# A second gate's modulation moved beside the output projection, and more seven-product pairs in a feed-forward block

## The chip, the cores and the metric

The kernel runs on one core of one Trainium2 chip. The metric is device time in microseconds (us) of one execution of the whole program. A core has a matrix engine (TensorE, "PE" in the profile, with its weight loads as "PEld"), a vector engine (VectorE, "DVE"), a scalar engine (ScalarE, "ACT"), GpSimd ("POOL") and SyncE ("SP"), which here does nothing but issue transfers. Each engine works through its own list of instructions in a fixed order, and engines wait for one another through semaphores.

## The reference

One decoder layer on 256 rows of width 2048, all in 32-bit floats. The parts that matter here:

```python
mod = jax.nn.silu(c) @ w_ada[l] + b_ada[l]
shift1, scale1, gate1, shift2, scale2, gate2 = jnp.split(mod[:, None, :], N_MOD, axis=-1)
h = rms_norm(x, norm1_gain[l]) * (1 + scale1) + shift1
x = x + gate1 * mixing_sublayer(h, ..., w_out[l])      # ends in  y @ w_out
h = rms_norm(x, norm2_gain[l]) * (1 + scale2) + shift2
gate, up = jnp.split(h @ w_ffn_in, 2, axis=-1)         # w_ffn_in is 2048 x 11264
x = x + gate2 * ((jax.nn.silu(gate) * up) @ w_ffn_out) # w_ffn_out is 5632 x 2048
```

`c` is one vector of 2048 numbers, `w_ada` is 2048 x 12288: each of the six segments of `mod` (here `gate2`) is a product of a vector with a 2048 x 2048 block of `w_ada`, 16 MB that are read once.

## The kernel before

**Products.** A 32-bit product is made of three passes of TensorE: both operands are split into a rounded high part and a low rest, and `mm3` (L163 to L166) adds high x high, high x low and low x high in the same PSUM bank. A pass takes a 128 x 128 stationary tile of the activations and streams 512 columns of weights. The 256 rows are two tiles `t` of 128.

**Weights.** `load_weights` (L135) brings two 128-row tiles of weights at a time, 512 KB, into one of four `raw` buffers (issued from SP, L146); ScalarE casts it to the high part `whi` (L158), VectorE subtracts to make the low part `wlo` (L159). There are four `whi` and four `wlo` buffers, and a caller may name further `spare` tiles. `block` (L168) then runs one column block of 512 over all row tiles of the weights. Where a block is called with `tiles=(0,)` and then `tiles=(1,)`, the weights of the whole block have to be there by the end of its first half.

**Background.** A segment of `mod` is done on VectorE: 32 loads of 128 x 1024 of `w_ada` into tiles of a ring (`ring["tags"]`), each followed by one multiply-add ("mac", L289, 128 x 1024). `tick` hands these out: `block` calls it at every second row tile with the number in `state["rate"]`, so a rate of 0.65 means 0.65 loads and macs per 512 KB of weights. A mac is recorded when the ring is full, behind the last `wlo` split recorded so far. `biased` (L366) clears the sum on GpSimd and puts the bias row into it.

**Order of the stages** around the change: mixing branches (`y_block`); the output projection with `w_out`, four blocks of 512 columns, the fourth one tile at a time, with `residual` (gate1 times the block, plus `x`), and the norm of the second half (`norm2_rows`, `norm2_turn`, its transposes at L1199); eleven feed-forward units, each 512 columns of `gate` and 512 of `up`; the output of the feed-forward, in a first pass over columns 0 to 1023 (`OUT_A`), a second pass over columns 1024 to 2047 (`OUT_B`), and plain blocks for the rows that the second pass leaves. Weights are loaded under `prio()`, that is, the planner that makes the fixed order prefers them to work recorded earlier without it.

**Seven-product pairs.** `fast_products` (L1328) takes two column blocks and pairs of row tiles. A plain pair is 2 x 2 x 2 = 8 products (24 passes). A pair marked 1 in the order list is done as a 2 x 2 block product with seven products (21 passes): sums and differences of the weights are made on VectorE (L1312) in two tiles of `tags`, each of them split like weights (L1309), and sums of the activations are made once beforehand (`sums_of_h2`, `sums_of_unit`, L1272). The units in `FAST` have three such pairs of eight, `OUT_A` has six of 22, `OUT_B` six of 14. `sums_of_unit(n)` (L1462) adds high and low part of one unit's activation (L1466), makes four sums (L1272) and splits them (L1470, L1471), in the tiles `AR0` and `AR1`; it is called at steps 2, 4 and 6 of the first pass.

**gate2** is appended to the background after the last fast unit, so it runs beside units 8, 9 and 10; what is left is flushed at step 7 of the first pass. `parts_of_gate2` and `rows_of_gate2` (L1483, L1489) spread it over all partitions near the end of that pass. The residual `x2` is written to memory after the projection (`put_away`) and read back at steps 8 to 11 of the first pass (`bring_back`).

## Time and profile before

| | us |
|---|---|
| median of 3 runs | 1591.57 |
| lowest, highest | 1590.14, 1591.96 |
| the profiled execution: its own time | 1590.96 |
| the profiled execution: span of the profile | 1589.2 |

Where stages lie in that span, from the timeline: the output projection from about 782 to 872, its fourth block from 848.6; unit 0 from 873; the fast units 1 to 7 from about 919 to 1216; units 8 to 10 to about 1350; the first output pass to 1468.5; the second to about 1541; the end at 1589.

The page gives busy time and share of the span by engine, then groups of instructions: the line, engine, operation, `out<-in` with the tiles' names, the shape, a count, and behind the bar the busy time, the mean duration of one in ns, and the idle time of the engine just ahead of them with what ended it. A row of the timeline is start, duration, engine, line, operation and names, with the idle time before it in brackets. A row of the windows is the stretch, its length, the busy time of PE, PEld, DVE, ACT and POOL with counts, the granted clock of TensorE, the mean busy share of the 16 DMA engines, and GB/s. A transfer's row is its count, its size and the median us from issue to landing. Passes of TensorE overlap: the duration of one is longer than the time from one start to the next.

### The profile page before, as it was taken

The page shows a single profiled execution, that of the slowest core. Times are in us where ns is not written, and L with a number is a line of the kernel's source. Part 1 is how long each engine was busy: PE and PEld are TensorE (multiplying, and loading weights), DVE is VectorE, ACT ScalarE, POOL GpSimd, SP SyncE. Part 2 cuts the span into 40 slices and gives each one's busy share as a digit, 9 for nine tenths or more (in the row PEclk, how much of TensorE's full clock was granted, in tenths as well). Part 3 has the DMA queues.
Part 4 walks back from the last instruction along what each step waited for, and adds up shares of the span by engine and source line. Part 5 has one row for each costly group of instructions (what it writes and reads, how often), then busy time and mean ns, then how long its engine had stood idle before and what let it go on. Part 6 is the DMA issues. An engine that isn't in the chain of part 4 may idle for free.

```text
span 1589.2 us, 20174 instructions
## 1 busy us (share of the span) xinstructions
PE 1577.6 (99%) x7243; PEld 1304.6 (82%) x7243; DVE 1299.3 (82%) x1556; ACT 852.6 (54%) x1195; POOL 11.2 (1%) x22
## 2 busy tenths in 40 slices
PE   9999999999999999999999999999999999999998
PEld 7878888888888888888887888888888888888887
DVE  6889996888888686877756689999997677998884
ACT  5654448775764444444445756555554434455552
POOL 1000000000000000000000000000000000000000
PEclk9999999999999999999999999999999999999999
DMA  9999997677788899988767566666668789866664
GB/s 334 360 328 322 333 305 241 212 229 231 231 267 271 300 300 324 307 278 298 230 206 244 174 195 189 198 202 196 206 191 279 259 290 311 275 193 219 201 207 138
DMA packets 195740, 400.16 MB, mean 252 GB/s; under 512 B 13038, under 2 KB 28052, under 8 KB 195640
## 3 DMA queue, kind: packets, MB, share of 16 engines
q1 hardware_dynamic: 194664, 396.70, 75.9%
q0 software_dynamic: 800, 2.11, 0.3%
q8 instruction: 57, 0.93, 0.2%
q14 instruction: 43, 0.35, 0.1%
q10 hardware_dynamic: 176, 0.07, 0.0%
HBM read 394.63 MB, written 4.19 MB: 251 GB/s over the span
## 4 chain that ended last, share of the span: by engine, by line
PE 88%; DVE 4%; ACT 3%; DMA 3%; issue 2%; SPq 0%; ACTq 0%; DVEq 0%
PE acc L166 22%; PE acc L165 21%; PE acc L164 21%; PE misc L165 6%; PE misc L166 6%; PE misc L164 5%; DMA raw<-w_in 2%; PE acc L443 1%; ACT whi L158 1%; DVE wlo L159 1%; DMA raw<-w_br_gla 1%; DVE wlo L1309 1%; PE misc L812 1%; PE misc L1122 1%; ACT scr L638 1%
## 5 line engine op out<-in xcount | busy, mean ns | idle before, releaser
L158 ACT CAST whi<-raw 128x1024 fp32r<-128x1024 f32 x362 | 368.5, 1022 | 406.0 <-PE acc L166 270.2
L159 DVE TENSOR_TENSOR wlo<-raw,whi 128x1024 fp32r<-128x1024 f32 x362 | 425.6, 1183 | 186.8 <-ACT whi L158 184.8
L164 PE MATMUL acc<-whi,H 128*128 128x512 f32 x1245 | 487.3, 392 | 1.2 <-ACT H L455 0.8
L165 PE MATMUL acc<-wlo,H 128*128 128x512 f32 x1245 | 486.3, 391 | 0.8 <-DVE wlo L159 0.7
L166 PE MATMUL acc<-whi,H 128*128 128x512 f32 x1245 | 486.0, 391 | 0.4 <-DVE H L462 0.4
L166 PEld LDWEIGHTS acc<-whi,H 128*128 128x128 f32 x1245 | 233.6, 188 | 50.7 <-DVE H L462 1.6
L164 PEld LDWEIGHTS acc<-whi,H 128*128 128x128 f32 x1245 | 233.7, 188 | 50.0 <-ACT H L455 1.3
L165 PEld LDWEIGHTS acc<-wlo,H 128*128 128x128 f32 x1245 | 233.9, 188 | 48.6 <-DVE wlo L159 1.7
L1308 ACT CAST whi<-raw 128x1024 fp32r<-128x1024 f32 (+1 forms) x148 | 142.0, 974 | 100.4 <-PE acc L166 37.0
L1309 DVE TENSOR_TENSOR wlo<-raw,whi 128x1024 fp32r<-128x1024 f32 (+1 forms) x148 | 162.8, 1122 | 10.9 <-ACT whi L1308 9.5
L165 PE MATMUL acc<-wlo,A 128*128 128x512 f32 x222 | 86.5, 390 | 0.8 <-DVE wlo L159 0.8
L164 PE MATMUL acc<-whi,A 128*128 128x512 f32 x222 | 87.0, 392 | 0.0
L166 PE MATMUL acc<-whi,A 128*128 128x512 f32 x216 | 84.1, 389 | 0.0
L289 DVE SCALAR_TENSOR_TENSOR ada<-AR,csil,ada 128x1024 f32<-128x1024 f32 x51 | 64.8, 1278 | 1.8 <-DMA AR<-w_ada 1.6
L164 PE MATMUL misc<-whi,H 128*128 128x512 f32 x158 | 61.7, 391 | 0.0
L165 PE MATMUL misc<-wlo,H 128*128 128x512 f32 x158 | 61.6, 390 | 0.0
L166 PE MATMUL misc<-whi,H 128*128 128x512 f32 x158 | 61.5, 389 | 0.0
L165 PEld LDWEIGHTS acc<-wlo,A 128*128 128x128 f32 x222 | 41.7, 188 | 9.5 <-DVE wlo L159 1.1
L164 PEld LDWEIGHTS acc<-whi,A 128*128 128x128 f32 x222 | 41.7, 188 | 8.6 <-ACT whi L158 0.3
L1308 ACT CAST A<-raw 128x1024 fp32r<-128x1024 f32 (+1 forms) x36 | 34.9, 982 | 25.5 <-DMA raw<-w_ffn_in 9.1
L1308 ACT CAST whi<-AR 128x1024 fp32r<-128x1024 f32 x24 | 25.3, 1053 | 42.1 <-PE misc L166 20.6
L166 PEld LDWEIGHTS acc<-whi,A 128*128 128x128 f32 x216 | 40.6, 188 | 8.5
(487 smaller groups left out, 2306.3 us busy)
## 6 DMA issues: line engine op xcount, KB each, us to landing
raw<-w_in SPq DMA_DIRECT2D x205, 512.0 KB, 5.0
raw<-w_ffn_in SPq DMA_DIRECT2D x176, 512.0 KB, 4.6
raw<-w_ffn_out SPq DMA_DIRECT2D x88, 512.0 KB, 5.1
AR<-w_ada SPq DMA_DIRECT2D x70, 512.0 KB, 5.0
raw<-w_out SPq DMA_DIRECT2D x32, 512.0 KB, 4.8
KC<-w_ada SPq DMA_DIRECT2D x26, 512.0 KB, 5.3
OS<-w_ada SPq DMA_DIRECT2D x16, 512.0 KB, 6.5
KD<-w_ada SPq DMA_DIRECT2D x16, 512.0 KB, 5.5
```

Source lines behind the costliest of these rows:

```text
L158: state["cast"] = nc.scalar.copy(hi[:, :n, :], raw[:, :n, :])
L159: state["split"] = nc.vector.tensor_tensor(lo[:, :n, :], raw[:, :n, :], hi[:, :n, :].bitcast(F32), op=ALU.subtract)
L164: nc.tensor.matmul(ps, lh, rh, start=start, stop=False, skip_group_check=seeded)
L165: nc.tensor.matmul(ps, lh, rl, start=False, stop=False, skip_group_check=seeded)
L166: state["mm"] = nc.tensor.matmul(ps, ll, rh, start=False, stop=stop, skip_group_check=seeded)
L289: nc.vector.scalar_tensor_tensor(acc, raw, c, acc, op0=ALU.mult, op1=ALU.add)
L443: state["warm"] = nc.tensor.matmul(ps, ones_r, wide, start=True, stop=True)
L638: nc.scalar.activation(junk, heads(b)[:, t, h, :], AF.Square, accum_out=ss[:, t, i : i + 1])
L812: nc.tensor.matmul(ps[:n, t * N_GLA + h, :].rearrange("p (s l) -> p s l", l=L), at(f, h, t)[:, :n], odd(at(f, h, t)), start=True, stop=True,)
L1122: nc.tensor.transpose(ps[:, i, :], src[:, i * P : (i + 1) * P], ident)
L1308: nc.scalar.copy(hi[:, :n, :], src)
L1309: state["split"] = nc.vector.tensor_tensor(lo[:, :n, :], src, hi[:, :n, :].bitcast(F32), op=ALU.subtract)
```

## The change

- The background work for `gate2` starts at the beginning of the output projection instead of after the last fast unit, at a rate of 0.68. Its sum lies in `OS0` and `T3` instead of `ada`; its ring is `A12`, `KD`, `KC` and at first `H7`, then `T0`. Through the fourth projection block and the first block of unit 0, which go one tile at a time, the rate is halved or nothing (`pace`). The finished sum is written to memory before the first fast unit and read back at step 7 of the first output pass.
- Units 2 to 10 are fast instead of 1 to 7: nine instead of seven.
- The second output pass has 18 pairs, eight of them fast, instead of 14 with six. It needs the activation sums of unit 3 as well, made at the last step of the first pass. The plain remainder is 8 row tiles instead of 16, and the last block has no spare tiles.
- Tiles move accordingly: the scratch tiles of the output passes are `AR0`, `A8`; the activations of units 8 and 9 lie elsewhere; spare tiles of the fourth projection block and of unit 0 are others; two quarters of `x2` come back after the second pass is recorded.

```diff
-RATE_IN, RATE_MID, RATE_FFN = 0.8, 0.6, 0.65
-RATE_OUT = 2.5
+RATE_IN, RATE_MID, RATE_LATE = 0.8, 0.6, 0.68
...
-FAST = range(1, 8)
-OUT_UNITS = (4, 5, 6)
+FAST = range(2, 11)
+OUT_UNITS = (4, 5, 6, 3)
...
-OUT_B = ((0, 0), (1, 0)) + tuple(x for i in range(6) for x in ((8 + i, 1), (2 + i, 0)))
+OUT_B = ((0, 0), (1, 0)) + tuple(x for a, b in zip((8, 9, 10, 11, 12, 13, 6, 7), (2, 3, 4, 5, 14, 15, 16, 17)) for x in ((a, 1), (b, 0)))
...
     def block(...
-              steps=None):
+              steps=None, pace=None):
...
+        if pace is None:
+            pace = 1.0 if tiles[-1] == NT - 1 else 0.0
         for k in range(k0, k1):
-            if (k - k0) % 2 == 0 and tiles[-1] == NT - 1:
-                tick(state["rate"])
+            if (k - k0) % 2 == 0:
+                tick(state["rate"] * pace)
...
-            hf = S(("KC", "T6")[j - 2], [P, 4, P]) if t == 0 and j >= 2 else scr([P, 4, P])
+            hf = S(("OD", "T6")[j - 2], [P, 4, P]) if t == 0 and j >= 2 else scr([P, 4, P])
...
-    def bring_back(n):
-        x2[n] = S(X2_TAGS[n], [P, NT, NB])
+    def bring_back(n, tag):
+        x2[n] = S(tag, [P, NT, NB])
...
+    gate2_away = [away.tile([P, 2 * NB], F32, tag=f"gate2_{j}", name=nm("gate2")) for j in range(2)]
+
+    def gate2_bg():
+        acc = biased([S(tag, [P, 2 * NB]) for tag in ("OS0", "T3")], SEG_GATE2)
+        yield from ada_segment_steps(acc, SEG_GATE2, None, False)
+        yield from last_macs()
+        for j in range(2):
+            nc.gpsimd.dma_start(gate2_away[j], acc[j])
+
+    state["rate"] = RATE_LATE
+    ring["tags"] = ("A12", "KD", "KC", "H7")
+    bg.append(gate2_bg())
...
-    w = load_weights(I["w_out"], 0, KC, 3 * NB, spare=("T0", "T3", "OS0", "OS1", "OS2", "OD", "A7", "A11"))
-    flush()
+    w = load_weights(I["w_out"], 0, KC, 3 * NB, spare=("T0", "AR0", "AR1", "OS1", "OS2", "OD", "A7", "A11"))
+    ring["tags"] = ("A12", "KD", "KC")
+    while SEG_SCALE2 not in mod2:
+        tick(1)
...
-        block({t: ps}, y_at, None, 0, KC, 0, w=w, tiles=(t,), steps={N2_AT[0]: lambda: norm2_turn(0, xs)} if t else None)
+        block({t: ps}, y_at, None, 0, KC, 0, w=w, tiles=(t,), steps={N2_AT[0]: lambda: norm2_turn(0, xs)} if t else None,
+              pace=0 if t else 0.5)
...
-             "OS0", "OS1", "OS2", "OD", "KD", "H0", "H1"]
+             "ada", "ada", "AR1", "A4", "H0", "H1"]
...
-    state["rate"] = RATE_FFN
-    ring["tags"] = ("AR0", "AR1", "KC")
+    ring["tags"] = ("A12", "KD", "KC", "T0")
     for i in range(NFF):
+        if i == FAST[0]:
+            flush()
+        if i == NFF - 1:
+            state["more_rooms"] = state["more_rooms"][:1]
...
-        if i == FAST[-1] + 1:
-            ring["tags"] = ("AR0", "AR1", "KC", "A2", "A3")
-            bg.append(gate2_bg())
...
-            w = load_weights(w_ff, 0, KC, 0, spare=("A12", "KD", "A9", "A10", "A0", "A1", "T1", "T2"))
+            w = load_weights(w_ff, 0, KC, 0, spare=("A9", "A10", "A0", "A1", "T1", "T2", "T4", "T5"))
...
-    CUT = KF - 14
+    CUT = 2 * len(OUT_B)
...
-        full = S("AR0", [P, 4, T])
+        full = S(OUT_TAGS[0], [P, 4, T])
...
-        sf = S("AR1", [P, 4, 2, P])
+        sf = S(OUT_TAGS[1], [P, 4, 2, P])
...
-    state["rate"] = RATE_OUT
-    hooks[7] = flush
+    def gate2_back():
+        state["gate2"] = [S(tag, [P, 2 * NB]) for tag in ("A2", "A3")]
+        for j in range(2):
+            nc.sync.dma_start(state["gate2"][j], gate2_away[j])
+
+    hooks[7] = gate2_back
...
-    for n in range(4):
-        hooks[8 + n] = lambda n=n: bring_back(n)
+    for n in range(2):
+        hooks[8 + n] = lambda n=n: bring_back(n, ("OS1", "OS2")[n])
...
-    hooks[behind + 2] = lambda: rows_of_gate2(1)
+    hooks[behind + 2] = lambda: (rows_of_gate2(1), sums_of_unit(3))
...
+    for n in (2, 3):
+        bring_back(n, f"H{n}")
-    REST = 2 * len(OUT_B)
+    REST = CUT
...
-    block(pss, act_at, w_fo, REST, CUT, n * NB, go_on=True, more=True, seeded=True)
-    w = load_weights(w_fo, CUT, KF, n * NB, spare=[f"H{j}" for j in range(2, 8)])
+    w = load_weights(w_fo, CUT, KF, n * NB)
```

28 lines of the change are left out of this document (14 added, 14 removed).

## The prediction

> **What bounds the kernel now.** The first view is the page: busy time by engine and the chain that ended last, by engine. The second is the list of waits, for TensorE alone (total us, times, longest).
>
> ```profile
> span 1589.2 us, 20174 instructions
> ...
> PE 1577.6 (99%) x7243; PEld 1304.6 (82%) x7243; DVE 1299.3 (82%) x1556; ACT 852.6 (54%) x1195; POOL 11.2 (1%) x22
> ...
> PE 88%; DVE 4%; ACT 3%; DMA 3%; issue 2%; SPq 0%; ACTq 0%; DVEq 0%
> ```
>
> ```profile
> PE misc L216 <- DMA H<-c: 2.6, 1, 2.6
> PE acc L165 <- DVE wlo L159: 1.4, 2, 0.8
> ...
> PE misc L165 <- DVE wlo L1309: 0.4, 1, 0.4
> ```
>
> TensorE is the bound nearly everywhere: 88% of the chain is its own work, and its longest wait, 2.6 us, is at the very start. So time goes down by passes left out, and up by whatever makes TensorE wait. What does a pass cost? The timeline of TensorE in a fast unit:
>
> ```profile
> 1000.16 0.39 PE L164 MATMUL acc<-A,H 128*128 128x512 f32 x1
> ...
> 1009.46 0.39 PE L166 MATMUL misc<-whi,H 128*128 128x512 f32 x1
> 1009.69 1.03 PE L1122 MATMUL acc<-ident,scr 128*128 128x128 f32 x8
> ```
>
> The first two are the first and the last of 42 passes without a gap: 9.30 / 41 = 0.2268 us from start to start. The 0.39 us that a row gives as duration overlaps its neighbours and is not the price. Third view, windows (stretch, length, busy PE, PEld, DVE, ACT, POOL, clock, transfer share, GB/s):
>
> ```profile
> 40.00:80.00 40.00, 40.00 (x178) 33.14 (x177) 34.13 (x34) 25.02 (x38) 0.00 (x0) 1.00 1.01 360
> ...
> 782.00:848.00 66.00, 66.00 (x300) 54.77 (x299) 38.13 (x41) 28.62 (x35) 1.10 (x2) 1.00 0.64 203
> ...
> 960.00:1000.00 40.00, 40.00 (x182) 33.19 (x181) 37.64 (x47) 23.05 (x26) 0.00 (x0) 1.00 0.62 197
> 1320.00:1360.00 40.00, 40.00 (x182) 33.22 (x181) 31.96 (x31) 16.54 (x18) 0.00 (x0) 1.00 0.95 322
> 1360.00:1400.00 40.00, 40.00 (x178) 33.07 (x177) 39.57 (x46) 20.13 (x20) 0.00 (x0) 1.00 0.69 220
> ```
>
> TensorE is full in all five, at the full clock, but what stands next to it differs: in fast units (960) VectorE with 37.64 of 40 us, in units with background (1320) the transfers with 0.95, at the head of the first output pass (1360) VectorE with 39.57. In the projection (782) both have room: 38.13 of 66, and 0.64. The change takes background out of a stretch where transfers are nearly full, makes VectorE nearly full there, and fills the projection's room.
>
> **Passes removed.** Two more fast units with three fast pairs each, and two more fast pairs in the second output pass: 8 pairs, each with 21 passes for 24. 8 x 3 x 0.2268 = **5.44 us** less. Transposes, `rows_of_gate2` and the plain products keep their number; `gate2`'s macs are on VectorE and cost TensorE nothing before or after.
>
> **Fast units 8 to 10** cost nothing beside that. Each is like the seven in the trace, and 960 to 1000 shows what covers the weight sums: 2.36 us of VectorE left per 40. Three such units in a row more do not change a balance that holds over seven. Unit 10 has one room less for split weights (five instead of six); the output passes work with four. If the cover went, lateness would show as a wait for L1309. The head of the first pass loses the last macs of `gate2` and gains unit 10's merges; I take 0.
>
> **The projection as the new place of 32 loads and macs.** The rows for it: transfers to landing, without background (window 782 to 848) and with it (1245 to 1350), and VectorE's prices.
>
> ```profile
> raw<-w_out SPq DMA_DIRECT2D x23, 512.0 KB, 4.6
> x<-A POOLq DMA_DIRECT2D x2, 512.0 KB, 5.0
> ```
>
> ```profile
> raw<-w_ffn_in SPq DMA_DIRECT2D x31, 512.0 KB, 6.1
> ```
>
> ```profile
> L159 DVE TENSOR_TENSOR wlo<-raw,whi 128x1024 fp32r<-128x1024 f32 x362 | 425.6, 1183 | 186.8 <-ACT whi L158 184.8
> ...
> L289 DVE SCALAR_TENSOR_TENSOR ada<-AR,csil,ada 128x1024 f32<-128x1024 f32 x51 | 64.8, 1278 | 1.8 <-DMA AR<-w_ada 1.6
> ```
>
> VectorE: a 512 KB piece of weights lasts 12 passes, 2.72 us; one split and 0.68 macs take 1.18 + 0.68 x 1.28 = 2.05 us of it. That fits. Transfers: three blocks are 288 passes, 65.3 us, and need 24 pieces, 24 x 0.68 = 16.3 loads of `w_ada` and about 2.5 pieces of `x2` written: 42.8 x 0.524 MB = 22.4 MB, or 344 GB/s. The row at 40 us carried 360, the one at 1320 carried 322 at a share of 0.95, which is 339 at a share of one. So the stretch is just full. The `w_ada` loads have four ring tiles, hence some 16 us to spare, and do not stop anything when they are late; weights are late by the queue only, for which I take the step from 4.6 to 6.1 us. The blocks that run both row tiles have a piece in hand for that, so 0 there.
>
> By the Trainium skill, DMA: Bandwidth & Descriptors, Specifications, HBM gives one core about 358 GB/s. The 360 of the row at 40 us agrees. By that figure 22.4 MB take 62.7 us, an estimate, and the projection would starve nobody; by the 339 worked out above they take 66.2, 0.9 us over.
>
> The fourth block is another matter: its 16 row tiles must be there within its first half, 48 passes, 10.9 us. Timelines of ScalarE, VectorE and TensorE there:
>
> ```profile
> 847.84 1.05 ACT L158 CAST T<-raw 128x1024 fp32r<-128x1024 f32 x1 [0.67 <-DMA raw<-w_out]
> ...
> 855.03 1.05 ACT L158 CAST A<-raw 128x1024 fp32r<-128x1024 f32 x1 [0.56 <-DMA raw<-w_out]
> ```
>
> ```profile
> 856.11 1.22 DVE L159 TENSOR_TENSOR A<-raw,A 128x1024 fp32r<-128x1024 f32 x1 [0.39 <-ACT A L158]
> 859.72 0.69 DVE L1176 TENSOR_TENSOR scr<-T,acc 128x512 f32<-128x512 f32 x1 [2.38 <-PE acc L166]
> ```
>
> ```profile
> 858.16 0.39 PE L164 MATMUL acc<-A,A 128*128 128x512 f32 x1
> 858.38 0.39 PE L165 MATMUL acc<-A,A 128*128 128x512 f32 x1
> ```
>
> Both casts wait for their transfer, and the second one's transfer could start only when the first piece was split and its buffer free. The last low part is ready at 857.33 and wanted at 858.38: 1.05 us in hand. If both transfers take 1.5 us longer, it is 3.0 - 1.05 = 1.95 us late; if they stay at 4.6, nothing. The rate is halved here, so I take **0.8**, between. Then the chain residual, norm, transposes, first pass of unit 0 runs through VectorE: a mac in front of it costs 1.28 us, two 2.56; the 2.38 us that VectorE idles ahead of 859.72 holds one. I take 0, the bounds are 0 and 2.56. `biased` makes SP wait for GpSimd's clear, behind which weights are queued:
>
> ```profile
> SPq L371 <- POOL ada L369: 4.0, 2, 3.4
> ```
>
> The longest such wait is 3.4 us now, four raw buffers of 2.72 us are ahead of it: 0. `gate2`'s way to memory and back are four pieces more, on GpSimd's queue before unit 2 and on SP at step 7, both away from full stretches: 0. The wait of the two late `bring_back` transfers on SP has only plain weights behind it: 0.
>
> **The sums of unit 3** are new work on VectorE, at the worst place, where the first output pass ends. Their price, from the lines of the other three units, and what stands there now, on VectorE and TensorE:
>
> ```profile
> L1466 DVE TENSOR_TENSOR AR<-T,T x2: 1224/1225/1226, 1376.9 to 1383.2; 128x1024 f32<-128x1024 f32 x2
> ```
>
> ```profile
> L1272 DVE TENSOR_TENSOR AR<-AR x6: 419/420/426, 1374.3 to 1388.1; 128x256 f32<-128x256 f32 x6
> ```
>
> ```profile
> L1471 DVE TENSOR_TENSOR H<-AR,H x3: 1217/1218/1219, 1379.2 to 1392.2; 128x1024 fp32r<-128x1024 f32 x3
> ```
>
> ```profile
> 1477.97 1.23 DVE L1309 TENSOR_TENSOR wlo<-AR,whi 128x1024 fp32r<-128x1024 f32 x1 [0.95 <-ACT whi L1308]
> 1480.69 1.23 DVE L1309 TENSOR_TENSOR wlo<-AR,whi 128x1024 fp32r<-128x1024 f32 x1 [1.50 <-ACT whi L1308]
> ```
>
> ```profile
> 1482.99 0.39 PE L165 MATMUL acc<-wlo,H 128*128 128x512 f32 x1
> ...
> 1484.90 0.50 PE L165 MATMUL misc<-wlo,A 128*128 128x512 f32 x1 [0.39 <-DVE wlo L1309]
> ```
>
> 1.22 + 4 x 0.42 + 1.22 = 4.12 us. They need `AR0`, which the first fast pair of the second pass wants next, so they cannot simply be put off. Idle there is 0.95 + 1.50, and the low part ready at 1481.92 is wanted at 1482.99, 1.07 in hand: 4.12 - 2.45 - 1.07 = **0.6 us** late. Bounds: 4.12, if all of it falls ahead of one split, and -0.4, if the wait at 1484.90 goes.
>
> **The tail.** The last block has no spare tiles now. Its last piece can be cast only when the block before ends; on VectorE the output adds of that block come first.
>
> ```profile
> 1562.72 1.28 DVE L1451 TENSOR_TENSOR scr<-ada,misc 128x512 f32<-128x512 f32 x2
> 1563.91 1.29 DVE L1453 TENSOR_TENSOR A<-A,scr 128x512 f32<-128x512 f32 x2
> ```
>
> 1.28 + 1.29 + 1.18 = 3.75 us against 19 passes, 4.31: 0, at most 1.
>
> **The sum**, against the profiled execution's own 1590.96 (span 1589.2, 1.8 around it): -5.44 + 0.8 + 0.6 = -4.0, so 1586.9. The median of the three runs is 1591.57, 0.6 above the profiled one; the prediction is for a median: **1587.5**.
>
> **Rivals.**
>
> - *No new wait.* TensorE never waited on VectorE for more than 0.8 us at once, and margins hold: 1591.57 - 5.44 = 1586.1. For it: units 8 to 10 carried 0.65 without a gap. Against: the two margins of about 1 us.
> - *Waits in place of passes.* All three places give half their bounds, 1.0 + 1.3 + 2.0 = 4.3: 1590.4. For it: VectorE has no idle stretch longer than 1.5 us where the new sums go.
> - *Transfers become the bound of the projection*, and the kernel gets slower. One mechanism: 22.4 MB do not go through in 65.3 us. It decides at 22.4 / (65.3 + 5.44) = 317 GB/s; at 300 the three blocks take 74.7 us, 9.4 more, and the kernel 1595.5. Against it: 322 GB/s with a share still under one, and 360.
> - *The change does not do what it says*: the passes go, but a fast unit follows VectorE's pace. At 37.64 of 40 this needs 6% more work on VectorE, and units 8 to 10 lose background instead. I give it no share of its own.
>
> **How the numbers follow.** Forecast 0.42, no new wait 0.22, waits in place of passes 0.27, transfers 0.09. A measurement here tells about 0.2%, 3.2 us, from no change, so faster means below 1588.4: the first two, 0.64. The third is within, 0.27; the last slower, 0.09. The range is 1585.2 to 1592.5: below, the full gain with the old wait at 1484.90 gone and 0.5 us of scatter; above, the third case with two thirds of its bounds, 5.7, and 0.6 of scatter. It leaves out the transfer case and the far ends.
>
> **What would show it.** The changed profile should have 24 passes fewer, bar lost records, units 8 to 10 each 9 x 0.2268 = 2.04 us shorter, a transfer share near 1 from 782 to 848 with TensorE still full, new PE waits for L159 near 858 and for L1309 near 1475, none in units 2 to 10. Wrong would be: waits of TensorE over 0.5 us inside the first three projection blocks (transfers), waits on L1309 inside units 8 to 10 (VectorE), or a wait at the end of the last block's first half (tail).

## The result: slower, and the profile after

| | before | after |
|---|---|---|
| median, us | 1590.86 (4 runs) | 1599.44 (4 runs) |
| lowest, highest | 1589.28, 1591.96 | 1597.79, 1601.38 |
| the profiled execution: its own time, span | 1590.96, 1589.2 | 1598.12, 1596.3 |

The ratio after to before is 1.0055, with a 95% interval of 1.0038 to 1.0073. The kernel is slower by 8.6 us, and lies outside the predicted range of 1585.2 to 1592.5.

The page of after: span, busy time by engine, and the chain that ended last.

```profile
span 1596.3 us, 20231 instructions
...
PE 1576.8 (99%) x7219; PEld 1301.2 (82%) x7219; DVE 1343.1 (84%) x1626; ACT 866.2 (54%) x1214; POOL 12.4 (1%) x24
...
PE 82%; DVE 7%; DMA 5%; ACT 3%; issue 2%; POOL 0%; ACTq 0%; DVEq 0%; POOLq 0%
```

The 24 passes are gone (7243 to 7219). In the chain TensorE's own work has fallen from 88% to 82%, VectorE has risen from 4% to 7% and transfers from 3% to 5%. Six hundredths of the span are some 95 us, far more than the 8.6 that were lost, so the chain says that more work now has no margin, not what that costs. The waits of TensorE (total us, times, longest) show new names:

```profile
PE acc L164 <- DVE wlo L1321: 2.1, 1, 2.1
PE misc L1200 <- DVE ada L1188: 2.0, 1, 2.0
PE acc L163 <- ACT H L1211: 1.4, 2, 1.1
...
PE misc L163 <- DVE misc L1355: 1.0, 1, 1.0
...
PE acc L164 <- DVE OS L158: 0.8, 1, 0.8
...
PE acc L163 <- DVE A L193: 0.7, 1, 0.7
```

They lie in four places: L158 in the fourth projection block, L1200 and L1211 in the norm behind it, L193 and L1355 in unit 2, L1321 in the first output pass. The windows that answer to those of before:

```profile
782.00:848.00 66.00, 66.00 (x299) 54.78 (x298) 50.51 (x52) 27.80 (x34) 2.06 (x3) 1.00 0.83 281
960.00:1000.00 40.00, 39.30 (x176) 31.83 (x175) 33.54 (x38) 20.50 (x23) 1.06 (x2) 1.00 0.62 204
1320.00:1360.00 40.00, 40.00 (x182) 33.22 (x181) 38.43 (x47) 23.68 (x26) 0.00 (x0) 1.00 0.67 234
1360.00:1400.00 40.00, 40.00 (x178) 33.12 (x177) 27.99 (x35) 17.96 (x20) 0.00 (x0) 1.00 0.57 190
```

The first three projection blocks and units 8 to 10 keep TensorE full, as forecast. Only 960 to 1000, unit 2, is not full.

The waits do not say what each stage lost, because later work can catch up or fall further behind. For that I take stage lengths from TensorE's timeline: the transposes of a unit's activation (L1122 before, L1123 after) mark each unit, and the first matmul of `rows_of_gate2` marks the end of the first output pass. The stages before the projection run the same code in all kernels and differ by up to 2 us from the execution of before that is shown, so a stage is compared by its own length. Length in us before, and the difference after:

| stage | before | after |
|---|---|---|
| P: projection from its first block, norm, unit 0 | 137.36 | +5.69 |
| unit 1 (plain in place of fast) | 42.39 | +2.02 |
| unit 2 (the first fast unit after) | 42.40 | +2.68 |
| units 3 to 10 (8 to 10 fast in place of plain) | 345.20 | -6.11 |
| F: first output pass up to the rows of `gate2` | 100.31 | +4.43 |
| E: from there to the end | 129.61 | -0.69 |

The sum is +8.0; the spans differ by 7.1, since the stages ahead were 0.7 us shorter in this execution of after and the last bit behind the last pass differs a little. Three stages, P, unit 2 and F, lose 12.8 us, and the removed passes give back less than half of it.

**Stage P.** VectorE in after, between the last two pieces of the fourth block and the norm rows:

```profile
860.36 1.28 DVE L290 SCALAR_TENSOR_TENSOR OS<-KD,csil,OS 128x1024 f32<-128x1024 f32 x1
...
863.00 0.68 DVE L1177 TENSOR_TENSOR scr<-T,acc 128x512 f32<-128x512 f32 x1
863.59 1.28 DVE L290 SCALAR_TENSOR_TENSOR T<-KC,csil,T 128x1024 f32<-128x1024 f32 x1
...
868.92 1.28 DVE L290 SCALAR_TENSOR_TENSOR OS<-H,csil,OS 128x1024 f32<-128x1024 f32 x1
...
871.46 1.27 DVE L290 SCALAR_TENSOR_TENSOR T<-A,csil,T 128x1024 f32<-128x1024 f32 x1
872.65 1.91 DVE L1188 TENSOR_SCALAR ada<-A,tiny,tiny 128x512 f32<-128x512 f32 x4
```

TensorE at the same place, in after:

```profile
870.94 0.39 PE L165 MATMUL acc<-A,A 128*128 128x512 f32 x1
873.33 3.30 PE L1200 MATMUL misc<-ident,ada 128*128 128x128 f32 x16 [2.01 <-DVE ada L1188]
876.90 0.59 PE L163 MATMUL acc<-whi,H 128*128 128x512 f32 x1 [0.27 <-ACT H L1211]
```

And before, VectorE's norm rows, then TensorE:

```profile
867.54 1.91 DVE L1187 TENSOR_SCALAR ada<-A,tiny,tiny 128x512 f32<-128x512 f32 x4
```

```profile
868.23 2.00 PE L1199 MATMUL misc<-ident,ada 128*128 128x128 f32 x16 [0.16 <-DVE ada L1187]
...
873.07 0.50 PE L164 MATMUL acc<-whi,H 128*128 128x512 f32 x1 [0.30 <-ACT H L1210]
```

Three macs stand between the block's residual (L1177) and the norm rows (L1188), one ahead of both. From the residual to the rows it is 9.65 us (872.65 - 863.00) where it was 7.82 before (867.54 - 859.72), so the macs between them cost 1.8. The residual itself is 4.0 us late, counted from the start of the stage (76.2 for 72.2 us). Before, the block's last 11 passes stand behind the 16 transposes, and run while ScalarE makes unit 0's first tile. In after the transposes stand behind the block's last product, with nothing to cover what follows. They wait 2.01 us for the rows, and take 3.30 us for 2.00: the clock record shows half the clock for 3.41 us from 873.7 on. Pass for pass against before, TensorE is 1.5 us late at the point where the fourth block's first half ended, 4.6 us late after the transposes of the first tile, and 5.7 us late after those of the second, at 890.

SyncE before, then SyncE after (a row: start, time from the first to the last issue, queue, line, tiles, count):

```profile
832.18 18.38 SPq L146 DMA_DIRECT2D raw<-w_out  x8
```

```profile
828.28 11.70 SPq L145 DMA_DIRECT2D raw<-w_out  x6
840.80 0.34 SPq L385 DMA_DIRECT2D A<-w_ada  x1
842.00 0.34 SPq L385 DMA_DIRECT2D KD<-w_ada  x1
844.33 0.33 SPq L385 DMA_DIRECT2D KC<-w_ada  x1
844.75 0.39 SPq L145 DMA_DIRECT2D raw<-w_out  x1
```

Before, pieces of `w_out` go out one by one from 832 on. After, between 840.0 and 844.7 none goes out: SyncE stands at loads of `w_ada`, which wait for macs to free their tiles. Its waits at such loads between 825 and 862, by what ended them (total us, times, longest):

```profile
SPq L385 <- DVE T L290: 6.3, 4, 2.0
SPq L385 <- DVE OS L290: 5.1, 4, 2.0
```

**Stage F.** VectorE of after in the third fast pair of the pass, then the same pair before, then TensorE in after:

```profile
1413.42 0.69 DVE L1324 TENSOR_TENSOR AR<-raw,raw 128x512 f32<-128x512 f32 x1 [2.79 <-DMA raw<-w_ffn_out]
1414.03 3.49 DVE L1321 TENSOR_TENSOR wlo<-raw,whi 128x1024 fp32r<-128x1024 f32 x3
```

```profile
1406.80 3.50 DVE L1309 TENSOR_TENSOR wlo<-raw,whi 128x1024 fp32r<-128x1024 f32 x3
1410.21 0.69 DVE L1312 TENSOR_TENSOR AR<-raw,raw 128x512 f32<-128x512 f32 x1
```

```profile
1415.30 0.50 PE L164 MATMUL acc<-wlo,T 128*128 128x512 f32 x1 [2.08 <-DVE wlo L1321]
...
1416.66 0.63 PE L163 MATMUL acc<-whi,T 128*128 128x512 f32 x1
1417.09 0.63 PE L164 MATMUL acc<-wlo,T 128*128 128x512 f32 x1
```

The first weight difference of a fast pair (L1324) needs both raw pieces. Before, it stands behind three plain splits; in after, VectorE's fixed order has it ahead of three plain splits that run at once when it is through. It waits 2.79 us for its transfer, the splits wait behind it, and TensorE waits 2.08 us for the first of them. Then passes start 0.43 us apart for 3.41 us.

### The profile page after: what moved, and what is told of

Its sections match the earlier page's. It is cut to its first block, busy times and chain, and to the rows that moved or that the text cites. A ratio compares the mean times of both kernels' runs of the same rounds, so it can differ in the third digit from the quotient of the medians.

```text
span 1596.3 us, 20231 instructions
## 1 busy us (share of the span) xinstructions
PE 1576.8 (99%) x7219; PEld 1301.2 (82%) x7219; DVE 1343.1 (84%) x1626; ACT 866.2 (54%) x1214; POOL 12.4 (1%) x24
## 4 chain that ended last, share of the span: by engine, by line
PE 82%; DVE 7%; DMA 5%; ACT 3%; issue 2%; POOL 0%; ACTq 0%; DVEq 0%; POOLq 0%
PE acc L165 20%; PE acc L164 20%; PE acc L163 20%; PE misc L163 6%; PE misc L164 6%; PE misc L165 6%; DMA raw<-w_ffn_in 2%; DVE wlo L158 2%; DVE wlo L1321 1%; ACT whi L157 1%; DMA raw<-w_in 1%; DMA raw<-w_ffn_out 1%; PE acc L444 1%; PE misc L813 1%; PE misc L1123 1%
## 5 line engine op out<-in xcount | busy, mean ns | idle before, releaser
L157 ACT CAST whi<-raw 128x1024 fp32r<-128x1024 f32 x325 | 329.4, 1018 | 353.0 <-PE acc L165 217.6
L158 DVE TENSOR_TENSOR wlo<-raw,whi 128x1024 fp32r<-128x1024 f32 x325 | 380.3, 1178 | 141.8 <-ACT whi L157 139.8
L163 PE MATMUL acc<-whi,H 128*128 128x512 f32 x1145 | 447.9, 392 | 2.6 <-ACT H L1211 1.4
L164 PE MATMUL acc<-wlo,H 128*128 128x512 f32 x1145 | 447.1, 391 | 0.8 <-DVE wlo L158 0.7
L165 PE MATMUL acc<-whi,H 128*128 128x512 f32 x1145 | 446.7, 391 | 0.4 <-DVE H L463 0.4
L163 PEld LDWEIGHTS acc<-whi,H 128*128 128x128 f32 x1145 | 215.1, 188 | 47.7 <-ACT H L1211 2.0
L165 PEld LDWEIGHTS acc<-whi,H 128*128 128x128 f32 x1145 | 214.8, 188 | 46.3 <-DVE H L463 1.6
L1320 ACT CAST whi<-raw 128x1024 fp32r<-128x1024 f32 (+1 forms) x177 | 168.7, 970 | 120.0 <-PE acc L165 40.6
L1321 DVE TENSOR_TENSOR wlo<-raw,whi 128x1024 fp32r<-128x1024 f32 (+1 forms) x177 | 193.3, 1117 | 16.1 <-ACT whi L1320 15.1
L163 PE MATMUL misc<-whi,H 128*128 128x512 f32 (+1 forms) x201 | 78.2, 389 | 1.0 <-DVE misc L1355 1.0
L164 PE MATMUL misc<-wlo,H 128*128 128x512 f32 (+1 forms) x201 | 78.0, 388 | 0.0
L165 PE MATMUL misc<-whi,H 128*128 128x512 f32 (+1 forms) x201 | 77.8, 387 | 0.0
L1321 DVE TENSOR_TENSOR A<-raw,A 128x1024 fp32r<-128x1024 f32 (+1 forms) x47 | 52.9, 1140 | 3.9 <-ACT A L1320 3.8
```

The costliest lines, as they stand in the source:

```text
L157: state["cast"] = nc.scalar.copy(hi[:, :n, :], raw[:, :n, :])
L158: state["split"] = nc.vector.tensor_tensor(lo[:, :n, :], raw[:, :n, :], hi[:, :n, :].bitcast(F32), op=ALU.subtract)
L163: nc.tensor.matmul(ps, lh, rh, start=start, stop=False, skip_group_check=seeded)
L164: nc.tensor.matmul(ps, lh, rl, start=False, stop=False, skip_group_check=seeded)
L165: state["mm"] = nc.tensor.matmul(ps, ll, rh, start=False, stop=stop, skip_group_check=seeded)
L1320: nc.scalar.copy(hi[:, :n, :], src)
```

## The experiments

Each run below was compared with runs of the kernel before on the same chip (medians 1589.87 to 1590.88). The table gives the median, the ratio to before with its 95% interval, and the stage differences as above. Without any new wait they would be 0 for P, 2.04 for unit 1 (nine passes), 0 for unit 2, -6.12 for units 3 to 10, 0 for F and -1.36 for E (six passes); where units 2 and 3 are plain, 2.04 for unit 2 and -4.08 for units 3 to 10.

| run | us | ratio | P | unit 1 | unit 2 | 3 to 10 | F | E |
|---|---|---|---|---|---|---|---|---|
| after | 1599.44 | 1.0055 (1.0038 to 1.0073) | 5.69 | 2.02 | 2.68 | -6.11 | 4.43 | -0.69 |
| no gate2 | 1590.49 | 1.0000 (0.9990 to 1.0009) | 0.18 | 2.05 | -0.01 | -6.11 | 3.33 | 0.69 |
| norm chain free | 1600.49 | 1.0060 (1.0045 to 1.0075) | 5.50 | 2.43 | 3.36 | -6.09 | 3.40 | 0.12 |
| differences in order | 1594.79 | 1.0029 (1.0020 to 1.0038) | 5.75 | 2.02 | 2.34 | -6.11 | 0.00 | -0.69 |
| both of these | 1595.88 | 1.0032 (1.0021 to 1.0043) | 6.55 | 3.21 | 2.40 | -6.09 | -0.03 | 0.02 |
| loads only | 1593.60 | 1.0022 (1.0013 to 1.0032) | 8.29 | 2.04 | 0.00 | -6.12 | -0.02 | 0.30 |
| macs only | 1590.77 | 1.0004 (0.9994 to 1.0013) | 6.70 | 2.05 | -0.03 | -6.09 | -0.01 | -0.59 |
| no gate2, in order | 1587.65 | 0.9981 (0.9971 to 0.9990) | 0.23 | 2.04 | 0.00 | -6.12 | -0.01 | 0.19 |
| macs only, chain free | 1587.34 | 0.9981 (0.9971 to 0.9990) | 1.43 | 2.04 | 0.00 | -6.12 | -0.01 | -0.51 |
| GpSimd loads, chain free | 1590.99 | 1.0004 (0.9995 to 1.0014) | 3.84 | 2.04 | 1.18 | -6.12 | -0.01 | 0.34 |
| GpSimd loads | 1598.21 | 1.0053 (1.0038 to 1.0068) | 11.15 | 2.04 | 0.00 | -6.12 | -0.02 | 0.84 |
| over four plain units | 1602.81 | 1.0081 (1.0066 to 1.0096) | 11.14 | 2.04 | 2.04 | -3.75 | -0.01 | -0.26 |
| the same without `H7` | 1593.86 | 1.0016 (1.0006 to 1.0025) | 2.35 | 2.02 | 2.03 | -3.46 | -0.02 | -0.57 |
| pause and trickle | 1592.01 | 1.0008 (0.9998 to 1.0017) | 4.31 | 2.06 | 1.94 | -5.03 | -0.03 | 0.66 |
| GpSimd, third block thin | 1592.91 | 1.0012 (1.0003 to 1.0021) | 1.77 | 2.02 | 3.32 | -6.11 | -0.01 | 0.03 |
| GpSimd, third block none | 1591.26 | 1.0002 (0.9993 to 1.0011) | 0.25 | 2.05 | 3.33 | -6.11 | -0.03 | 0.21 |
| GpSimd, done by unit 2 | 1589.87 | 0.9996 (0.9987 to 1.0005) | 2.55 | 2.86 | 1.68 | -6.09 | -0.05 | 0.13 |
| GpSimd, both | 1590.57 | 1.0005 (0.9995 to 1.0014) | 0.34 | 2.28 | 2.58 | -6.12 | -0.01 | 0.23 |

The stages come from one execution of each kernel, the medians from 4 to 11. The sum of a row's stages and its ratio agree within 1.8 us, but for "pause and trickle" (2.6), whose profiled execution was the slowest of its ten (1596.0).

### Which parts lose: no gate2, norm chain free, differences in order, both

```diff
     def gate2_bg():
...
-        yield from ada_segment_steps(acc, SEG_GATE2, None, False)
-        yield from last_macs()
+        yield
```

> The changed kernel without the 32 loads of w_ada and the 32 macs of gate2 (gate2 is then the bias row alone); all else stays. My theory: the changed kernel gains its 5.44 us of passes and loses about 13 us in new waits at three places, of which the projection with unit 0 (5.7 us by the traces) and the first fast unit (2.7 us) come from gate2's work there, and the first output pass (4.4 us) does not. Then this runs 8.4 us below the changed kernel, about 1591, with the wait of the first output pass still there. Rival: gate2's work costs little, and the loss is spread by other tiles and rooms; then it stays above 1596.

```diff
-    ring["tags"] = ("A12", "KD", "KC", "H7")
+    ring["tags"] = ("A12", "KD", "KC")
...
-              pace=0 if t else 0.5)
+              pace=0)
...
+    state["rate"] = 0.76
     ring["tags"] = ("A12", "KD", "KC", "T0")
```

> The same loads and macs, but none handed out in the fourth projection block (pace 0, a ring of three tiles in the projection), the rate 0.76 from unit 0 on to make up for it. My theory: the wait of 2.4 us ahead of the norm's transposes near 870 comes from macs that stand between residual and norm on VectorE, and the stretch at half clock after it is its consequence; both go, 3.5 to 4 us, so about 1595.5. Rival: the transfers of w_ada make the weights late there and the chain is late for that; then the wait stays, and the time is within 1.5 us of the changed kernel's 1599.4.

```diff
-            sub(ta[:, 0], r1[:, 0], r0[:, 0])
-            sub(ta[:, 1], r1[:, 1], r1[:, 0])
+            with tc.issue_after(state["split"].ins) if not state.get("more_rooms") else nullcontext():
+                sub(ta[:, 0], r1[:, 0], r0[:, 0])
+                sub(ta[:, 1], r1[:, 1], r1[:, 0])
```

> Of the changed kernel only the planner's order is changed, in the two output passes: the two first weight differences of a seven-product pair may not stand ahead of the split of that pair's first piece on VectorE. My theory: the wait of 2.5 us near 1413 comes from a difference that waits for its transfer at the head of VectorE's list, with splits behind it whose pieces are there; with the stretch at half clock that follows this is about 4.2 us, so about 1595. Rival: the pieces are late because of the four pieces that come back from memory at the head of that pass, or because there are only four rooms; then the order changes nothing and it stays within 1 us of 1599.4.

> Both edits, the norm's chain kept free and the differences in order. If the two losses are separate, the gains add up: about 8 us below the changed kernel, 1591 to 1592. If the half-clock stretches are set by something else than the waits before them, one stays and it is 1593 or more.

Without `gate2`'s loads and macs, P and unit 2 lose nothing and F still loses 3.33. With the differences in order F loses 0.00. VectorE in that run, in the same place:

```profile
1410.41 3.50 DVE L1321 TENSOR_TENSOR wlo<-raw,whi 128x1024 fp32r<-128x1024 f32 x3
1413.83 0.68 DVE L1324 TENSOR_TENSOR AR<-raw,raw 128x512 f32<-128x512 f32 x1
```

The three splits now run first, and the difference finds its pieces there. So F is settled: it was an order on VectorE, not VectorE's load, and has nothing to do with `gate2`. P is not: freeing the norm chain of macs changed nothing (5.50), alone or with the other edit (6.55). My theory of that moment, the macs ahead of the norm rows, fell in the form in which I held it. In "both" the rows do follow the residual sooner, after 7.35 us for 10.03 in "differences in order" (7.82 before). But the residual is still 4.4 us late in its stage, and only 5 passes stand behind the transposes instead of 11.

### Transfers or VectorE: loads only, macs only, neither

All of these have the differences in order; the third has the edit of "no gate2" besides.

```diff
+            c = slice(0, 8) if state.get("thin") else slice(None)
-            ada_mac(acc[j], raw, k, zero)
+            ada_mac(acc[j][:, c], raw[:, c], k, zero)
...
+        state["thin"] = True
```

> The changed kernel with the two first weight differences of the output pairs behind their split (as in the run that put them there, 1594.8 us), and gate2's 32 products made over 8 of 1024 columns each, so most of gate2 is left out: all 32 loads of w_ada stay, in their places, and VectorE's time for them goes (from some 2.2 us each to a fixed cost). Transfers theory (the loads hold up the pieces of w_out and w_ffn_in, VectorE's time is not what is short): the second norm turn still comes 4 us or more later than before, and the time stays at 1592.5 to 1595.5 us. VectorE theory (the products stand in the way of splits and of the norm chain): the second norm turn comes within 1 us of before, the time 1587 to 1589.5 us.

A mac takes 1.28 us in the traces, not the 2.2 of this text; over 8 columns it took 0.22.

```diff
-                raw = araw([P, 2 * NB])
+                raw = state.get("one") or araw([P, 2 * NB])
...
-                with prio():
-                    nc.sync.dma_start(raw, w_ada[k * P : (k + 1) * P, c0 : c0 + 2 * NB])
+                if raw is not state.get("one"):
+                    with prio():
+                        nc.sync.dma_start(raw, w_ada[k * P : (k + 1) * P, c0 : c0 + 2 * NB])
...
+        one = state["one"] = S("A12", [P, 2 * NB])
+        nc.sync.dma_start(one, w_ada[:P, SEG_GATE2 * D : SEG_GATE2 * D + 2 * NB])
```

> The same kernel with all 32 products in full, but each of them reads one tile of w_ada that is loaded once, so 31 of the 32 loads are left out and gate2 is that of one tile 32 times over. Transfers theory: the second norm turn comes within 1.5 us of before, the time 1587 to 1590 us, with what is left of the loss at the first fast unit. VectorE theory: the second norm turn comes 4 us or more later than before, 1593 to 1596 us.

> Both suspects gone at once: gate2's loads and products left out (gate2 is its bias row alone) and the two first weight differences of the output pairs behind their split. Both losses that the runs so far show are out of it, so by the sum the removed passes should show in full: 5.4 us less than before less the 0.6 to 1.4 us of the starts and ends of the output passes, 1585.0 to 1587.0 us. If it stays at 1589 us or more, there is a third loss that hid behind the two.

In P both theories got what they asked for. With loads alone P loses 8.29, with macs alone 6.70, with neither 0.23. The loss in P has two causes, each enough by itself, and in these traces they do not add up (5.7 together). The ratios, over many executions, say it less sharply: against the run with neither, loads cost 6.5 us, macs 3.7 and both 7.6, of which 2.3 are in unit 2, each to about 2 us. So "macs only" ended below the 1593 to 1596 of the VectorE theory. "No gate2, in order" missed its forecast too, 1587.65 for 1585.0 to 1587.0: what is missing there is in E, 0.19 where six passes fewer give -1.36.

What the two causes look like differs. TensorE's waits in P, loads only, then macs only:

```profile
PE acc L163 <- ACT T L157: 2.7, 1, 2.7
PE acc L164 <- DVE wlo L158: 2.2, 2, 1.4
PE acc L163 <- ACT whi L157: 0.8, 1, 0.8
```

```profile
PE acc L163 <- ACT H L1212: 3.4, 1, 3.4
PE misc L1201 <- DVE ada L1189: 0.7, 1, 0.7
```

Loads alone make weights late (casts L157 and splits L158): pass for pass, TensorE is 6.2 us late at the point where the fourth block's first half ended before. Macs alone lose nothing up to there, and make the norm late (5.9 us by unit 0's first passes). This explains why freeing the chain did nothing while the loads were there: late weights took its place. The combination predicts that with no loads the free chain does pay, which the next run tried (macs only, with the edits of "norm chain free").

> The run with all products but one load (1590.8 us), with no product handed out in the fourth block and three instead of four pending. That run lost about 4 us between the first norm turn and the second. If the products ahead of the norm rows on VectorE made this (through the transposes, which then stood behind the block's last product with nothing to cover ScalarE's work), it goes: the second norm turn within 1.5 us of before and the time 1586.5 to 1588.5 us, as with no gate2 at all. If the products cost VectorE time that is short elsewhere, it stays at 1590 us or more.

P is 1.43 and the time 1587.34, as forecast. TensorE in that run:

```profile
866.36 2.00 PE L1201 MATMUL misc<-ident,ada 128*128 128x128 f32 x16 [0.16 <-DVE ada L1189]
868.11 0.48 PE L164 MATMUL acc<-OD,A 128*128 128x512 f32 x1
...
870.48 0.39 PE L165 MATMUL acc<-A,A 128*128 128x512 f32 x1
871.58 0.50 PE L163 MATMUL acc<-whi,H 128*128 128x512 f32 x1 [0.72 <-ACT H L1212]
```

The transposes stand ahead of the block's last 11 passes again, 2.5 us that cover ScalarE's work; with the macs, in after and in "macs only", they stood behind all of them. So macs ahead of the norm rows cost more than 1.28 us each: the transposes move behind the products, and the cover goes too. I take the reason for that order to be that the planner sees the rows late; an order with the macs in place and the transposes kept ahead was not tried. Unit 2 loses nothing with loads alone or macs alone. Both together need not cost there either (0.00 in "GpSimd loads" below, after a P that is 11.15 longer), so what makes unit 2 late stays open.

### What the loads do: SyncE's queue or bandwidth

Both runs have the differences in order; the first has the chain free as well.

```diff
-                    nc.sync.dma_start(raw, w_ada[k * P : (k + 1) * P, c0 : c0 + 2 * NB])
+                    (nc.gpsimd if seg == SEG_GATE2 else nc.sync).dma_start(raw, w_ada[k * P : (k + 1) * P, c0 : c0 + 2 * NB])
```

> The run with ordered differences and the norm chain clear (1595.9 us), with gate2's 32 loads of w_ada issued by GpSimd instead of SyncE: the same bytes at the same places in the program, but no piece of w_out or w_ffn_in waits behind a load that has no free tile. Queue theory: the pieces of the fourth block come in time, the second norm turn within 1.5 us of before, 1586.5 to 1589.5 us, faster than both kernels. Bandwidth theory: the pieces are as late as ever, 1593 us or more.

> The run with ordered differences alone (1594.8 us), with gate2's loads issued by GpSimd: the norm chain still has its products ahead of it. Queue theory: the late weights go, what the products do to the norm chain stays, so the time is that of the products alone (1590.8 us): 1589.5 to 1592.5 us, the second norm turn still 4 us or more late. Bandwidth theory: 1593.5 us or more.

Between the two forecasts: with the chain free, the other queue brings the ratio from 1.0032 down to 1.0004, 4.5 us for the same bytes. So SyncE's list, in which `w_out` stands behind loads without a free tile, was a large part. It was not all: P still loses 3.84, with gaps of TensorE of 0.73 and 2.05 us at 853. With the chain not free the time, 1598.21, is in the range of the bandwidth theory, but not for its reason. P is 11.15, worse than with SyncE. There VectorE has four macs around the block's residual from 859.50 on, a fifth at 867.83, and TensorE waits twice in the norm, 2.42 and 3.42 us. Why the macs bunch there stays open. GpSimd issued the loads of those four between 841.25 and 847.11, ahead of the `put_away` in its list that waits for a residual (857.61), so that transfer did not hold them up.

### Other places for gate2's 32 steps

All of these have the differences in order. First, as many fast units as before, and the steps thinner over a longer stretch:

```diff
-RATE_IN, RATE_MID, RATE_LATE = 0.8, 0.6, 0.68
+RATE_IN, RATE_MID, RATE_LATE = 0.8, 0.6, 0.46
...
-FAST = range(2, 11)
+FAST = range(4, 11)
...
-              pace=0 if t else 0.5)
+              pace=0)
...
-                block(pg, h2_at, None, 0, KC, 0, w=w, tiles=(t,), steps=None if t else {N2_AT[1]: lambda: norm2_turn(1, xs)}, pace=0.5 * t)
+                block(pg, h2_at, None, 0, KC, 0, w=w, tiles=(t,), steps=None if t else {N2_AT[1]: lambda: norm2_turn(1, xs)}, pace=0)
```

> Units 2 and 3 plain again (as many fast units as before, 4 to 10), gate2's 32 steps spread thinner over the projection's first three blocks and units 0 to 3 (rate 0.46 for 0.68, none in the two blocks that run their tiles apart), differences ordered as above; eight fast pairs in the second output pass stay. It has 6 passes fewer than before (1.36 us). Transfers theory: at this rate the projection's blocks ask for some 300 GB/s, below the 340 to 360 that they get when full, so most of the loss goes: 1588.5 to 1590.5 us, the second norm turn within 2 us of before. VectorE theory (products in the first three blocks and in unit 0 cost what they cost at the higher rate, in proportion): 1591.5 to 1593 us.

```profile
916.71 1.28 DVE L290 SCALAR_TENSOR_TENSOR OS<-H,csil,OS 128x1024 f32<-128x1024 f32 x1
918.02 0.69 DVE L1212 TENSOR_TENSOR H<-T,H 128x512 fp32r<-128x512 f32 x1
```

This is VectorE in that run, which missed both forecasts. I had paused the background with a loaded tile of `w_ada` still in `H7`. The mac that frees it came in unit 0's second half, and the low part of `h2` that has to be written to `H7` (L1212) came behind it. TensorE stood for 4.27 us there, from one start to the next (3.88 of them idle). The next run only takes `H7` out of the ring.

```diff
-    ring["tags"] = ("A12", "KD", "KC", "H7")
+    ring["tags"] = ("A12", "KD", "KC")
```

> The run with gate2 over four plain units (1602.8 us) with one thing changed: its ring of loads no longer uses H7, the buffer that the last low half of h2 needs. In that run a product that had not been handed out yet held H7 until unit 0's second half, and TensorE waited 4.27 us there for that low half. If that slip was what made it slow, the time falls to 1588.5 to 1591.5 us and the second norm turn and unit 0's turn come within 2 us of before. If thinner loads simply don't help, it stays at 1595 us or more.

P falls from 11.14 to 2.35, so the slip was most of it: the gap and the stretch at half clock behind it are 5.6 of these 8.8 us, the rest went with the other ring. The time stays above the forecast: P keeps 2.35, units 3 to 10 lose 0.6, and no fast unit is gained against before.

"Pause and trickle" keeps nine fast units and three ring tiles, with `pace=0` around the norm:

```diff
-RATE_IN, RATE_MID, RATE_LATE = 0.8, 0.6, 0.68
+RATE_IN, RATE_MID, RATE_LATE = 0.8, 0.6, 0.66
...
-        block(pss, y_at, I["w_out"], 0, KC, n * NB)
+        block(pss, y_at, I["w_out"], 0, KC, n * NB, pace=(1.2, 1.2, 0.5)[n])
...
+    state["rate"] = 0.6
...
-        if i == FAST[0]:
+        if i == 1:
+            ring["tags"] = ("A12", "T0")
+        if i == 2:
+            state["rate"] = 0.14
+        if i == 4:
             flush()
```

> Nine fast units as in the changed kernel, differences ordered, and gate2's 32 steps placed around the norm: thicker in the projection's first two blocks (where the transfer share still was 0.65 to 0.79), thin in the third, none in the two blocks that run their tiles apart, 0.6 in unit 0's second half and unit 1, the last 4 or 5 in units 2 and 3 at about two a unit, where VectorE has some 2.4 us a unit to spare. If the loss is set where the weights of the fourth block and the norm chain meet the loads and products, this keeps the removed passes: 1586.5 to 1589.5 us, faster than both kernels. If the loss only moves on (transfers full in unit 1, VectorE full in units 2 and 3), 1591 us or more, with new waits there.

It fell: P still loses 4.31. No load is issued in the fourth block, but SyncE stood at a load until 845.79 and the last five pieces of `w_out` followed from 847.42. Units 2 and 3 lose 1.94 and 1.1 on top. The last four take GpSimd's queue and the free chain, with no step in unit 0's first half:

```diff
-        block(pss, y_at, I["w_out"], 0, KC, n * NB)
+        block(pss, y_at, I["w_out"], 0, KC, n * NB, pace=(1.3, 1.3, 0.3)[n])
```

The next three have (1.5, 1.2, 0), (1.5, 1.3, 0.1) and (1.6, 1.2, 0) there, and from unit 0 on a rate of 0.8, 1.2 and 1.2 for 0.76.

> As the run at 1591.0 us, with gate2's loads thicker in the projection's first two blocks (7 a block for 5.4), 1.6 in the third, none in the fourth and in unit 0's first half, 0.76 from unit 0's second half on. If bandwidth at the end of the third block sets the rest, the waits at 853 fall from 2.8 us to under 1, and the time to 1587 to 1589.5 us, faster than both kernels. If the loss moves on into units 0 to 2 (transfers full there), 1590.5 us or more with waits after 925.

> The same with no step handed out in the third block at all (8.2 and 6.5 in the first two, 0.8 from unit 0's second half on). By the bandwidth account it does as well as or better than the run before at 853 (waits under 0.6 us) and pays, if at all, in units 0 to 2: 1587 to 1590 us. If the late pieces stay with no load near them, bandwidth isn't the rest.

> As the run at 1591.3 us, with gate2's last 18 steps handed out faster (1.2 for 0.8 from unit 0's second half on, and one more step in the second and third block), so that all 32 products stand before the first weight difference of unit 2 on VectorE. If the leftovers made unit 2's loss, its waits of 3.7 us at 993 to 1007 go, units 2 to 10 cost what they cost with no gate2, and the time falls to 1587.5 to 1589.5 us, faster than both kernels. If the transfers of units 0 and 1 are full by then (8.4 MB in 21.8 us would be 385 GB/s), the waits come there instead and it stays at 1590.5 us or more.

> The last run with no step in the third block (8.7 and 6.5 in the first two) and 1.2 from unit 0's second half on. If the two parts are separate, the waits at 853 go (as with no step there: 0 against 3.0 us) and unit 2 loses no more than in the last run (1.7 us): 1587 to 1589 us, faster than both kernels. If the same bytes must show up somewhere in this stretch, it stays at 1589.5 us or more, with waits in unit 0's second half or unit 1.

Windows of the third and the fourth block, with GpSimd loads and the chain free, then with none handed out in the third block:

```profile
826.00:848.00 22.00, 22.00 (x98) 18.22 (x98) 18.96 (x18) 9.77 (x12) 3.19 (x6) 1.00 0.96 338
848.00:860.00 12.00, 10.10 (x43) 7.81 (x43) 8.85 (x11) 6.14 (x9) 1.07 (x2) 1.00 0.92 315
```

```profile
826.00:848.00 22.00, 22.00 (x99) 18.22 (x98) 16.75 (x17) 9.77 (x12) 2.65 (x5) 1.00 0.98 359
848.00:860.00 12.00, 12.00 (x54) 9.93 (x54) 8.97 (x11) 6.40 (x9) 0.54 (x1) 1.00 0.83 284
```

With no new loads behind 838, TensorE is full again in the fourth block (12.00 for 10.10 of 12 us) and P is 0.25. The transfers show why: two pieces of `w_out` issued between 843 and 848 have a median of 8.7 us from issue to landing with the loads, 4.6 without. So the rest of P is what the loads take from the transfers at the end of the third block and in those 12 us. The macs of these loads left with them, and no run here parts the two on GpSimd's queue. The steps have to go somewhere, though: unit 2 then loses 3.33, and VectorE there shows a leftover mac ahead of a split of a fast pair:

```profile
995.25 1.28 DVE L290 SCALAR_TENSOR_TENSOR T<-A,csil,T 128x1024 f32<-128x1024 f32 x1
996.45 1.22 DVE L1321 TENSOR_TENSOR wlo<-KD,whi 128x1024 fp32r<-128x1024 f32 x1
```

With the macs handed out faster unit 2 loses half of that, P 2.55 and unit 1 0.8. Both together gave 1590.57, not the 1587 to 1589 that I expected. A gain was forecast for each of the four by the account that I held; none came, and all end within 0.2% of before. No version that computes all of `gate2` was found faster than before; the two without its loads and without products ahead of the norm rows are (0.9981).

## Why the prediction was wrong, step by step

- **Passes removed, 5.44: right.** Units 3 to 10 are shorter by 6.11 (27 x 0.2268 = 6.12), unit 1 longer by 2.02. The second output pass's six are inside E, see below.
- **Fast units 8 to 10 cost nothing: right.** No wait there, VectorE at 38.43 of 40.
- **"The head of the first pass ... I take 0": right at the head, failed for the pass**, 4.43. I had weighed VectorE's amount of work, and the window at the head shows even less of it than before (27.99 for 39.57). The loss came 55 us later, where I had no term. What counted was the order: a difference waiting for a transfer at the head of VectorE's list. One edit that puts it behind a split removes all of it.
- **Three projection blocks, 0: right in TensorE** (66.00 of 66). But "do not stop anything when they are late", said of the loads of `w_ada`, **failed**: they stop SyncE (11.4 us of waits between 825 and 862), and through it the pieces behind them. Moving them to GpSimd was worth 4.5 us where the norm chain was free of macs. "The stretch is just full" was not so on the average: 281 GB/s at a share of 0.83, where I had 344, with 11 loads of `w_ada` issued in it for my 16.3. But five of them were issued within 9 us, from 840.80 to 849.59, around its end.
- **Fourth block, late weights, 0.8: right in part.** TensorE loses 1.5 there, inside my bound of 1.95; two gaps, 1.20 and 0.50 us from start to start where 0.23 is usual, make 1.24 of it. But I had slower transfers alone, 6.1 us for 4.6. The block's last pieces took up to 6.8 us, and were also issued 1.9 to 2.5 us later in the stage, for SyncE's list. And I had no term for the norm chain starting late with them, 4.0 us. With loads alone the waits there and in unit 0 add up to 5.7.
- **"A mac in front of it costs 1.28 us ... I take 0, the bounds are 0 and 2.56": failed.** The macs between residual and rows cost 1.8 us in after, inside the bound, but TensorE loses 4.2 in the norm, the 5.69 of P less the 1.5 of the fourth block. I counted the mac's duration and not what the fixed order does with the transposes, nor the stretch at half clock. Macs alone cost 6.70 in P, 3.7 by the ratios. Together with the step above, P lost 5.69 where I had 0.8.
- **Unit 2** had no term at all; I wrote that no wait would show in units 2 to 10. It lost 2.68, with the last three macs between its first splits and its pieces late (2.21 us of VectorE at a difference, 982.32). Which of these makes it is not shown.
- **Sums of unit 3, +0.6, with six passes off the second output pass: right in after, by luck in part.** -1.36 + 0.6 = -0.76, and E is -0.69. The wait of 0.39 at 1484.90 became 0.45 and 0.22 at 1491 and 1492, for casts of weight sums and pieces on ScalarE; the first of these casts had waited 2.69 us for VectorE, which made its weight sums behind the sums of unit 3. Other runs with nine fast units have E up to +0.84, so the two terms can't be told apart.
- **`biased`, the way to memory and back, the tail, 0: right.** TensorE has no gap behind 1492.

Of the rivals, "waits in place of passes" named fourth block and norm, but priced them at 2.3 us together, less than half of what they cost, and had nothing for F. The slower one, transfers, decided at the wrong place: it asked whether the three blocks as a whole get 317 GB/s. They got 281 with TensorE full, and the harm came in the 12 us behind them, where a whole block's weights have to come in half its time.

## What to carry to other kernels

Background work fits a stage only if it fits the narrowest stretch of it: ask what each queue's next instruction waits for at that place, for the issuing engine's list as much as for VectorE's. When two causes meet at one place, taking out one can show little or nothing; make the runs with each alone before dropping a theory. An instruction that waits for a transfer costs what is queued behind it, so put the splits whose data is there ahead of it.

## What was not expected of the hardware

From the projection to the last pass, TensorE's clock record shows stretches at half the clock, 3.413 us or twice that, in which passes start 0.43 us apart for 0.2268: eight passes in 3.41 us, about 1.6 us lost. In the runs they followed gaps, from one start to the next, of 2.36, 2.40, 2.47, 2.81, 3.10, 3.68, 3.80 and 4.27 us, and twice two shorter gaps close together (1.24 and 1.26; 2.16 and 1.26). Single gaps of 1.86 to 2.32 us were not followed by one. They are not what set P, though: "differences in order" has none there, with a gap of 2.20, and loses the same 5.75. The Trainium skill, TensorE: Matmul & The Clock Gate, Why this matters for your kernels, warns of gaps over about 3 us. Part 1 of the same page of the Trainium skill gives about 3.4 us as the window of the clock gate. The stretches of 3.413 us here agree with that, but they come after gaps from 2.36 us on (1.97 us of them idle).

The Trainium skill, DMA: Bandwidth & Descriptors, Issuing engines are not separate DMA queues, says that issuing from several engines saves only the time to start a transfer, since all share the same 16 DMA engines. The gaps of 0.73 and 2.05 us left at 853 with GpSimd's queue agree with the second half. The 4.5 us that the queue brought do not contradict the first, but show how large that saving gets when the issuing engine waits in its list for a tile to come free.
